# Two layers of a hybrid attention block: projection work spread evenly over the attention steps, some operations cut smaller, and the forget bias folded into a score product

## The chip, the cores and the metric

The kernel runs on one core of one Trainium2 chip. The metric is the time of one execution on the device in microseconds (us); before the change the median of three runs is 1368.33 us (1368.0 to 1369.17). One more execution was taken by the hardware profiler; its own time is 1369.85 us. The engines are called as in the profile: PE (matrix products; PEld is its loading of the stationary operand), DVE (vector), ACT (activations), POOL (GpSimd), SP (which here issues the transfers).

## The reference

Two layers over 512 tokens of width 1024, all in float32. Each layer is a mixer of three parallel head groups, then a gated MLP with a causal convolution:

```python
proj = h @ w_in      # split into fq fk fv ff | nq kc vc ks vs kw vw ng | dq dk dv
log_f = log_sigmoid(ff + b_forget); c = cumsum(log_f)
# forgetting attention ("fox"), 4 heads of width 64
s = q @ k.T * ATTN_SCALE + c_q[:, None] - c_k[None, :]
o_fox = masked_softmax(s, kpos <= qpos) @ v
# sparse attention, 8 heads: o = g0*compressed + g1*selected + g2*window
k_cmp = gelu(windows(kc) @ w1) @ w2          # the same for v_cmp
# dilated attention, 4 heads
mix = concat(o_fox, o_nsa, o_dil); x = x + rms_norm(mix @ w_out)
x = x + rms_norm((silu(conv(h @ w_up)[a]) * conv(h @ w_up)[b]) @ w_down)
```

The row term c_q drops out of a softmax, so a kernel needs only the term c_k, one value per head and key.

## The kernel before

**Numbers in two parts.** Every operand of a product is split into a high part, made by an ACT copy into a type of reduced precision, and a low part, made by a subtraction on DVE or POOL. A product is then three products on PE: high by high, low by high and high by low. `part_weights` (L137) does this for the weights: a weight tile `raw` arrives in one of three buffers, ACT writes `wh`, DVE or POOL writes `wl`. Names in `DCUTS` (L42: `w1`, `wo`) have each of the two operations cut in two along the slabs of the tile; the weights `wo2` (rows 512 to 1023 of the output projection, one slab of 1024 columns each) and the first weight of the MLP, `up` 0 0, are done in one operation of 1024 columns.

**The fox scores.** The query tile `q` of two heads holds the high part in partitions 0 to 63 and the low part in 64 to 127. The key tile `k` of a head holds the high part of the key twice (partitions 0 to 63 and 64 to 127) as plane 0 and the low part twice as plane 1 (`k_evac`, L494). So two products over 128 partitions give all terms. For fox heads a third product adds the forget bias: `esel` (a constant that picks a head) by `cst`, whose rows 0 to 3 and 32 to 35 hold the high and low parts of c for the four heads, the other rows zero:

```python
            mm(S[:, 0:n], qs, k[:, 0, 0:n], t != 1, False)
            mm(S[:, 0:n], qs, k[:, 1, 0:n], False, not fox)
            if fox:
                mm(S[:, 0:n], esel[:, u["h"], :], cst[:, 0:n], False, True)
```

`cst` is written once in a layer, by ACT and DVE (L612, L613), from a product `pcs` that stands on PE right after the projection of the fox queries (`fq_proj`, L594).

**Units, slots and pieces.** Attention is a pipeline of 96 units a layer: 16 fox units, 64 of the sparse group (8 heads, two branches), 16 dilated ones; a unit is one head, one branch and one block of 128 queries, and has 128, 256, 384 or 512 keys. One slot of the loop (L1238) starts one unit's scores and does later stages of earlier units: the masked minimum on DVE (1 slot later), the exponent on ACT, the normalization on POOL, the transposes on PE (4 slots), the copies `ph` on ACT and `pl` on DVE out of the transposes (5), the products with the values (7) and the head's output (7). Into the slots the loop puts pieces of other PE work, in a fixed order (`main_pieces`): 8 projections of 8 pieces (`kc`, `ks`, `nq0`, `kw`, `nq1`, `dv`, `dq`, `dk`), 8 pieces `w1` of the compression, and 16 pieces of the first half of the output projection (`out_first`), 88 in all. The second half (`out_start`) waits until the last unit has started, but each step in which it waits counts as a piece too. Five pieces go ahead of slot 0 (`FIRST`). Then a budget says how many follow in each slot; `until` calls more at once where a unit needs a projection that isn't there yet:

```python
        RATE = [1.4] * 12 + [0.8] * 98
...
                budget += RATE[i]
                while budget >= 1.0:
                    budget -= 1.0
                    if live[0] or pieces.late:
                        step()
                chain_step()
```

`chain_step` moves the compressed branch on by one stage a slot (`cmp_pieces`, L938): its gelu needs a reciprocal of 128x256 values, done as two operations of 128 columns in one stage (L952).

**Order.** PE's instructions keep the order in which the program writes them. DVE, ACT, POOL and SP are ordered by a planner at build time: by program order among what it expects to be ready. On the chip each engine then runs its list in that order and waits where an operand is late. Weight loads go out on SP as a raw buffer comes free. Large tiles (`q`, `k`, values, partial outputs) share 24 buffers (`NBIG`, L26). PSUM has two buffers `pt` for the transposes; a new transpose needs the copies `ph` and `pl` out of an older one to be done.

Of the kernel before, what the change touches and what calls it, by code (L numbers as in the profile page):

```python
# [10 lines left out]
F32R = mybir.dt.float32r  # L11
# [27 lines left out]
TT = "pt"  # L39
CT = "acc"  # L40
FIRST = 5
DCUTS = ("w1", "wo")  # L42
EV = (1, 3, 1, 1)
ORDER = (0, 1, 2, 4, 3, 5, 6, 7, 8)
HA0 = (1, 3)
# [29 lines left out]
def tile_hybrid_block(  # L75
# [61 lines left out]
    def part_weights(raw, nk, ncol, spare, tagn, pool, cut):  # L137
        DCUT = ((0, 2), (2, 4)) if cut else ((0, 4),)
        if spare:
            hi, lo = bt([128, nk, ncol], F32R, "wh"), bt([128, nk, ncol], F32R, "wl")  # L140
        else:
            hi = wpool.tile([128, nk, ncol], F32R, tag="wh", name=nm("wh" + tagn))
            lo = wpool.tile([128, nk, ncol], F32R, tag="wl", name=nm("wl" + tagn))
        for a, e in HCUT if pool else DCUT:
            ks = slice(nk * a // 4, nk * e // 4)
            nc.scalar.activation(hi[:, ks], raw[:, ks], AF.Copy)  # L146
        if pool:
            for a, e in PCUT:
                ks = slice(nk * a // 4, nk * e // 4)
                nc.gpsimd.tensor_sub(lo[:, ks], raw[:, ks], f(hi)[:, ks])  # L150
        else:
            for a, e in DCUT:
                ks = slice(nk * a // 4, nk * e // 4)
                nc.vector.tensor_sub(lo[:, ks], raw[:, ks], f(hi)[:, ks])  # L154
        return hi, lo

    plan, ready = [], {}
# [44 lines left out]
    def getw(*key, ahead=AHEAD, pre=None, peek=False):  # L202

        i = where[key]
        pre = ahead if pre is None else min(pre, ahead)
        tag = lambda k: "_".join(str(z) for z in k)
        for n in range(len(done)):
            upto = i + (ahead, pre)[n]
            while done[n] < len(plan) and done[n] <= upto:
                k, srcs, nk, ncol, spare = plan[done[n]]  # L210
                if n == 0:
                    ready[k] = load(srcs, nk, ncol, tag(k))
                else:
                    ready[k] = part_weights(ready[k], nk, ncol, spare, tag(k), k[1] in ONPOOL or k[1:4] in ONPOOL or k[0:3] in ONPOOL,
                                            k[1] in DCUTS)
                done[n] += 1
        return None if peek else ready.pop(key)

# [229 lines left out]
    for l in range(DEPTH):  # L448
# [42 lines left out]
                                               op0=ALU.mult, op1=ALU.subtract)  # L491
            return q

        def k_evac(p):  # L494
            k = bt([128, 2, 512], F32R, "k")
            nc.scalar.activation(k[:, 0, :], p, AF.Copy)
            nc.vector.tensor_sub(k[:, 1, :], p, f(k[:, 0, :]))
            return k

        def new_v(nh=2):  # L500
# [39 lines left out]
            tl.append(d.rearrange("p h u d -> p (h u d)"))  # L540
        tmode.__exit__(None, None, None)
        store["fv"] = fv
        store["fk"] = [k_evac(t_block(tl, 128 * j)) for j in range(4)]
        cpar = small.tile([128, 2, 88], F32, tag="cpar", bufs=1, name=nm("cpar"))
        crow = rt((88, 2, 128))
        for j in range(3):
# [47 lines left out]
        def fq_proj(c):  # L594
            hi, lo = getw(l, "fq", c, ahead=2)
            p = ps("acc")
            for k in range(KT):
                mm(p, hi[:, k, :], HH(k), k == 0, False)
                mm(p, hi[:, k, :], HL(k), False, False)
                mm(p, lo[:, k, :], HH(k), False, k == KT - 1)  # L600
            store["fq"].append(q_evac(p))

        fq_proj(0)
        fq_proj(1)
# [6 lines left out]
                       False, False)  # L611
        nc.scalar.activation(cst[0:4, :], pcs[0:4, :], AF.Copy)  # L612
        nc.vector.tensor_sub(cst[32:36, :], pcs[0:4, :], f(cst[0:4, :]))  # L613
        if l == 0:

            dint = rt(dt=I32)
            nc.gpsimd.iota(dint, pattern=[[-1, 512]], base=384, channel_multiplier=1)
            dflt = rt()
            nc.vector.tensor_copy(dflt, dint)
            cmask = const.tile([128, 512], F32, name="cmask")  # L620
            nc.vector.tensor_scalar(cmask, dflt, 0.0, BIG, op0=ALU.is_lt, op1=ALU.mult)
            dmask = const.tile([128, 512], F32, name="dmask")
            cnt = rt()
            nc.vector.tensor_scalar(cnt, dflt, 128.0, None, op0=ALU.is_le)
            for m in (3, 15):
                mi = rt(dt=I32)
                nc.vector.tensor_scalar(mi, dint, m, None, op0=ALU.bitwise_and)
                mf = rt()
                nc.vector.tensor_copy(mf, mi)
                nc.vector.scalar_tensor_tensor(cnt, mf, 0.0, cnt, op0=ALU.is_equal, op1=ALU.add)  # L630
            ge0 = rt()
            nc.vector.tensor_scalar(ge0, dflt, 0.0, None, op0=ALU.is_ge)
            nc.vector.tensor_mul(cnt, cnt, ge0)
            nc.vector.tensor_scalar(dmask, cnt, 0.0, BIG, op0=ALU.is_equal, op1=ALU.mult)
            for v, lg in ((2.0, -math.log(2.0)), (3.0, -math.log(3.0))):
                t = rt()
                nc.vector.tensor_scalar(t, cnt, v, lg, op0=ALU.is_equal, op1=ALU.mult)
                nc.vector.tensor_add(dmask, dmask, t)

            ci = rt((128, NST, 32))  # L640
            nc.gpsimd.iota(ci, pattern=[[128, NST], [-16, 32]], base=-31, channel_multiplier=1,
                           allow_small_or_imprecise_dtypes=True)
            cvalid = const.tile([128, NST, 32], F32, name="cvalid")
            nc.vector.tensor_scalar(cvalid, ci, 0.0, None, op0=ALU.is_ge)
            cinv = const.tile([128, NST, 32], F32, name="cinv")
            nc.vector.tensor_scalar(cinv, ci, 0.0, BIG, op0=ALU.is_lt, op1=ALU.mult)

            odd = const.tile([128, 2], F32, name="odd")
            oi = small.tile([128, 1], I32, tag="oi", bufs=1, name="oi")
            nc.gpsimd.iota(oi, pattern=[[0, 1]], base=0, channel_multiplier=1)  # L650
            nc.vector.tensor_scalar(oi, oi, 32, None, op0=ALU.bitwise_and)
            nc.vector.tensor_copy(odd[:, 1:2], oi)
            nc.vector.tensor_scalar(odd[:, 0:1], odd[:, 1:2], 0.0, None, op0=ALU.is_equal)
            nc.vector.tensor_scalar(odd[:, 1:2], odd[:, 1:2], 0.0, None, op0=ALU.is_gt)
            vcm = const.tile([128, 2, 2, 2, 64], F32R, name="vcm")
# [1 line left out]
        nc.vector.tensor_scalar(gates, gates, 1.0, None, op0=ALU.add)  # L657
        nc.vector.reciprocal(gates, gates)

        mix, sums = {}, {}  # L660
        OFIRST = (0, 1, 2, 3)

        def split_mix(k, eng, cs=slice(0, 512)):
            if k not in mix:
                if k != 7:
                    mix[k] = bt([128, 2, 512], F32R, "mix")
                else:
                    mix[k] = ptp.tile([128, 2, 512], F32R, tag="ph", name=nm("mix"))
            d = mix[k]
            nc.scalar.activation(d[:, 0, cs], sums[k][:, cs], AF.Copy)  # L670
            eng.tensor_sub(d[:, 1, cs], sums[k][:, cs], f(d[:, 0, cs]))

# [265 lines left out]
        def cmp_pieces(xc, w2r):  # L938
# [9 lines left out]
            nc.scalar.activation(t2, t1, AF.Exp, scale=-2.0 * math.sqrt(2.0 / math.pi))  # L948
            yield
            nc.vector.tensor_scalar(t2, t2, 1.0, None, op0=ALU.add)  # L950
            for c in range(2):
                nc.vector.reciprocal(t2[:, 128 * c:128 * c + 128], t2[:, 128 * c:128 * c + 128])  # L952
            yield
            nc.gpsimd.tensor_mul(xc, xc, t2)
            yield
            yield
# [146 lines left out]
        def st_scores(u):  # L1103
            t = u["t"]
            n = u["n"] = 128 * (t + 1)
            q, k, u["v"], u["mask"], u["gate"] = operands(u)
            if t != 1:
                state["s"] = ps("s")
            S = u["S"] = state["s"][:, 128 * (t == 1):]
            qs = q[:, 128 * t:128 * t + 128]  # L1110
            fox = u["grp"] == "f"
            mm(S[:, 0:n], qs, k[:, 0, 0:n], t != 1, False)
            mm(S[:, 0:n], qs, k[:, 1, 0:n], False, not fox)
            if fox:
                mm(S[:, 0:n], esel[:, u["h"], :], cst[:, 0:n], False, True)

        def st_max(u):
            n = u["n"]
# [109 lines left out]
                mm(p[:, sl], hi[:, k, :], HL(k)[:, sl], False, False)  # L1228
                mm(p[:, sl], lo[:, k, :], HH(k)[:, sl], False, last and k == KORDER[-1])

        RATE = [1.4] * 12 + [0.8] * 98
        LM, LN, LT, LE, LV, LO = LAGS
        stages = ((0, st_scores), (LE, st_keep_hi), (LM, st_max), (LN, st_norm), (LE, st_keep_lo), (LM, st_exp),
                  (LV, st_values), (LT, st_turn), (LO, st_out))
# [2 lines left out]
        with tc.manual_schedule(engines={mybir.EngineType.PE}):  # L1237
            for i in range(FIRST):  # L1238
                step()
            for i in range(len(units) + LO):  # L1240
                slot[0] = i
                U = lambda lag: units[i - lag] if 0 <= i - lag < len(units) else None
                for lag, fn in stages:
                    if U(lag) is not None:
                        fn(U(lag))
                budget += RATE[i]
                while budget >= 1.0:
                    budget -= 1.0
                    if live[0] or pieces.late:
                        step()  # L1250
                chain_step()
                if store.get("pc") and whole and whole[0][1] <= i:
                    cmp_values(whole.pop(0)[0])
# [169 lines left out]
```

## Time and profile before

| what | value |
|---|---|
| median of three runs | 1368.33 us |
| the profiled execution: its time, its span | 1369.85 us, 1367.9 us |
| PE, PEld busy | 98 %, 86 % of the span |
| DVE, ACT, POOL busy | 62 %, 53 %, 21 % |
| PE share of the chain of work that ended last | 85 % |
| mean granted clock of PE | 0.998 of full |
| the slots of layer 1, of layer 2 | 62 to 302 us, 737 to 979 us |

The span runs from the first to the last instruction of the program; 1.95 us of the profiled execution's time lie around it. A busy time is the time in which an instruction of that engine is under way. Products on PE overlap, so the time that one costs is the distance from its start to the start of the next, not its duration. The granted clock is a share of 2.4 GHz.

### The profile page before, as it was taken

The numbers are of one execution on the slowest core, as the hardware profiler recorded it, in microseconds if no ns is written. First come the engines' busy times: TensorE is split into PE (matmuls) and PEld (weight loads), VectorE is DVE, ScalarE is ACT, GpSimd is POOL, SyncE is SP. The second block draws the span as 40 slices with busy tenths as digits, with TensorE's granted clock in tenths as the row PEclk, the third lists the DMA queues.
The fourth block names the chain that finished last, engine by engine and source line by source line (L and its number), as shares of the span: only waits on it lengthen the run. The fifth ranks groups of instructions, "written<-read, shape, count | busy, mean of one in ns | idle before, by whom it ended". The sixth has DMA issues, their size and how long they took to land.

```text
span 1367.9 us, 21028 instructions
## 1 busy us (share of the span) xinstructions
PE 1338.0 (98%) x7855; PEld 1177.9 (86%) x7855; DVE 850.4 (62%) x1893; ACT 728.2 (53%) x1506; POOL 287.0 (21%) x343
## 2 busy tenths in 40 slices
PE   9999999999999999999999999999999999999997
PEld 8899998978888888888898999999798888888886
DVE  7677787677755555433464887777876555554334
ACT  6567767777533333333465677667774333333232
POOL 2364753341000000000004647634210000000000
PEclk9999999999999999999999999999999999999999
DMA  6323311131333333333333242111323333332231
GB/s 181 94 63 115 104 35 48 58 128 33 107 93 103 97 92 96 104 93 123 111 96 93 63 139 63 47 41 58 120 62 98 103 92 93 104 97 92 94 122 62
DMA packets 145517, 123.74 MB, mean 90 GB/s; under 512 B 8264, under 2 KB 135688, under 8 KB 145416
## 3 DMA queue, kind: packets, MB, share of 16 engines
q1 hardware_dynamic: 145416, 122.40, 29.5%
q8 instruction: 62, 1.02, 0.3%
q14 instruction: 39, 0.32, 0.1%
HBM read 118.19 MB, written 4.19 MB: 89 GB/s over the span
## 4 chain that ended last, share of the span: by engine, by line
PE 85%; DVE 7%; ACT 4%; POOL 2%; issue 2%; DMA 0%; SPq 0%; ACTq 0%; POOLq 0%; DVEq 0%
PE acc L115 39%; PE s L115 19%; PE pt L115 13%; PE o L115 10%; PE pt L1156 3%; POOL wt L795 1%; PE pt L737 1%; DVE hl L271 1%; DVE pl L1172 1%; DVE r L1126 1%; ACT r L1131 1%; DVE x L913 0%; ACT hh L270 0%; ACT h L310 0%; ACT ph L1167 0%
## 5 line engine op out<-in xcount | busy, mean ns | idle before, releaser
L154 DVE TENSOR_TENSOR wl_up<-raw_up,wh_up 128x1024 fp32r<-128x1024 f32 x78 | 95.6, 1225 | 170.8 <-ACT wh_up L146 170.8
L146 ACT ACTIVATE wh_up<-raw_up 128x1024 fp32r<-128x1024 f32 (+1 forms) x90 | 89.6, 1001 | 160.4 <-PE acc L115 68.1
L154 DVE TENSOR_TENSOR wl_wd<-raw_wd,wh_wd 128x1024 fp32r<-128x1024 f32 x42 | 51.5, 1225 | 133.7 <-ACT wh_wd L146 133.7
L146 ACT ACTIVATE wh_wd<-raw_wd 128x1024 fp32r<-128x1024 f32 x42 | 44.5, 1060 | 144.8 <-PE pt L115 135.5
L1143 POOL TENSOR_SCALAR r<-r,sm,gates 128x128 f32<-128x128 f32 (+3 forms) x128 | 86.4, 683 | 126.1 <-DVE sm L1139 82.3
L1131 ACT ACTIVATE r<-r,sm 128x128 f32<-128x128 f32 x192 | 106.7, 557 | 9.3 <-DVE sm L1126 8.4
L115 PE MATMUL acc<-hh,wl_up 128*128 128x512 f32 (+1 forms) x272 | 102.4, 376 | 0.0
L115 PE MATMUL acc<-hl,wh_up 128*128 128x512 f32 (+1 forms) x272 | 102.4, 376 | 0.0
L115 PE MATMUL acc<-hh,wh_up 128*128 128x512 f32 (+1 forms) x272 | 102.4, 376 | 0.0
L150 POOL TENSOR_TENSOR wl_kc<-raw_kc,wh_kc 128x512 fp32r<-128x512 f32 x8 | 11.8, 1490 | 417.6 <-ACT wh_kc L146 416.8
L115 PE MATMUL s<-k,q 128*128 128x512 f32 (+3 forms) x384 | 96.2, 337 | 0.6 <-DVE sm L1126 0.6
L1172 DVE TENSOR_TENSOR pl<-pt,ph 128x384 fp32r<-128x384 f32 x144 | 85.6, 596 | 17.3 <-ACT ph L1167 15.9
L1167 ACT ACTIVATE ph<-pt 128x384 fp32r<-128x384 f32 x144 | 75.4, 523 | 29.1 <-PE pt L1156 27.9
L1126 DVE CUSTOM_DVE_ANT_0 r<-s,cmask 128x128 f32<-128x128 f32 (+3 forms) x160 | 76.0, 482 | 20.6 <-PE s L115 16.2
L1156 PE MATMUL pt<-ident,r 128*128 128x128 f32 x480 | 77.5, 276 | 7.0 <-DVE pl L1172 5.5
L115 PE MATMUL acc<-wh_wd,gh 128*128 128x512 f32 x252 | 83.7, 389 | 0.0
L115 PE MATMUL s<-hh,wh_up 128*128 128x512 f32 (+1 forms) x224 | 80.4, 359 | 0.0
L115 PE MATMUL s<-hl,wh_up 128*128 128x512 f32 (+1 forms) x224 | 80.4, 359 | 0.0
L115 PE MATMUL s<-hh,wl_up 128*128 128x512 f32 (+1 forms) x224 | 80.4, 359 | 0.0
L1347 ACT ACTIVATE r<-r 128x512 f32<-128x512 f32 x44 | 27.8, 632 | 85.7 <-DVE r L1328 85.5
L1156 PEld LDWEIGHTS pt<-ident,r 128*128 128x128 f32 x480 | 55.4, 141 | 15.9 <-POOL r L1143 6.8
L115 PE MATMUL acc<-wh_wo,mix 128*128 128x256 f32 (+1 forms) x296 | 67.6, 305 | 0.0
(439 smaller groups left out, 4121.2 us busy)
## 6 DMA issues: line engine op xcount, KB each, us to landing
raw_up<-in_w_up_dram SPq DMA_DIRECT2D x88, 512.0 KB, 3.8
raw_wd<-in_w_down_dram SPq DMA_DIRECT2D x44, 512.0 KB, 3.4
raw_wo<-in_w_out_dram SPq DMA_DIRECT2D x16, 512.0 KB, 3.5
x<-in_x_dram SPq DMA_DIRECT2D x8, 512.0 KB, 5.9
raw_nq<-in_w_in_dram SPq DMA_DIRECT2D x8, 512.0 KB, 3.7
raw_w<-in_cmp_w_k_dram SPq DMA_DIRECT2D x8, 512.0 KB, 4.0
raw_w<-in_cmp_w_v_dram SPq DMA_DIRECT2D x8, 512.0 KB, 4.2
raw_fk<-in_w_in_dram SPq DMA_DIRECT2D x4, 512.0 KB, 5.9
```

The costliest lines, as they stand in the source:

```text
L115: nc.tensor.matmul(o, lhsT=lhsT, rhs=rhs, start=start, stop=stop, skip_group_check=True)
L146: nc.scalar.activation(hi[:, ks], raw[:, ks], AF.Copy)
L154: nc.vector.tensor_sub(lo[:, ks], raw[:, ks], f(hi)[:, ks])
L271: nc.vector.scalar_tensor_tensor(lo, src, gain[:, k:k + 1], f(hi), op0=ALU.mult, op1=ALU.subtract)
L737: nc.tensor.transpose(p[:, 128 * s:128 * s + 128], tl[s][:, 128 * j:128 * j + 128], ident)
L1126: nc.vector.tensor_tensor_reduce(row[:, 0:n], u["S"][:, 0:n], u["mask"][:, 512 - n:512], op0=ALU.add, op1=ALU.min, scale=1.0, scalar=3.0e3 ...
L1131: nc.scalar.activation(row[:, 0:n], row[:, 0:n], AF.Exp, scale=-1.0, bias=sm_[0], accum_out=sm_[1])
L1143: nc.gpsimd.tensor_scalar(row[:, 0:n], row[:, 0:n], z["sm"][2], g_, op0=ALU.mult, op1=ALU.mult)
L1156: nc.tensor.transpose(p[:, 128 * c:128 * c + 128], blocks[z], ident)
L1167: nc.scalar.activation(hi, src, AF.Copy)
L1172: nc.vector.tensor_sub(*u["lo"])
L1347: nc.scalar.activation(cd[0], cd[0], AF.Silu)
```

## The change

- The fox keys' low part is written in partitions 0 to 63 only (`k_evac(p, 64)`); 64 to 127 of plane 1 take a copy of rows 0 to 63 of `cst` by a transfer, one for each of the four heads. Two new large tiles `fq2` hold the high part of the query (copied by a transfer) in partitions 0 to 63 and `esel` of the head in 64 to 127 (two transfers each, which repeat a row of 128 values four times). The second score product of a fox unit takes `fq2`, and the third goes. The product of the two low parts, which the second had held for fox heads, goes with it.
- `RATE` is replaced: 1.4 for the first 12 slots as before, then the pieces that are left divided by the units that are left.
- `wo2` and `up` 0 are cut in two operations each on ACT and DVE; a tile of one slab is cut by columns.
- The reciprocal is done as four operations of 64 columns, one stage of the chain each.
- `kept` and `OLAG` are written and not used.

```diff
-DCUTS = ("w1", "wo")
+DCUTS = ("w1", "wo", "wo2")
...
+        def cutting(z, a, e):
+            return z[:, nk * a // 4:nk * e // 4] if nk > 1 else z[:, :, ncol * a // 4:ncol * e // 4]
+
         for a, e in HCUT if pool else DCUT:
...
+            nc.scalar.activation(cutting(hi, a, e), cutting(raw, a, e), AF.Copy)
+        for a, e in PCUT if pool else DCUT:
+            (nc.gpsimd if pool else nc.vector).tensor_sub(cutting(lo, a, e), cutting(raw, a, e), cutting(f(hi), a, e))
...
-                                            k[1] in DCUTS)
+                                            k[1] in DCUTS or k[1:3] == ("up", 0))
...
-        def k_evac(p):
+        def k_evac(p, low=128):
...
-            nc.vector.tensor_sub(k[:, 1, :], p, f(k[:, 0, :]))
+            nc.vector.tensor_sub(k[0:low, 1, :], p[0:low], f(k[0:low, 0, :]))
...
-        store["fk"] = [k_evac(t_block(tl, 128 * j)) for j in range(4)]
+        store["fk"] = [k_evac(t_block(tl, 128 * j), 64) for j in range(4)]
+        fq2 = [bt([128, 2, 512], F32R, "q2") for _ in range(2)]
...
-            store["fq"].append(q_evac(p))
+            q = q_evac(p)
+            store["fq"].append(q)
+            nc.sync.dma_start(f(fq2[c])[0:64], f(q)[0:64])
+            for j in range(2):
+                nc.sync.dma_start(f(fq2[c])[64:128, j].rearrange("p (t n) -> p t n", t=NST),
+                                  bc(f(esel)[0:64, 2 * c + j, :], 1, NST))
...
         nc.vector.tensor_sub(cst[32:36, :], pcs[0:4, :], f(cst[0:4, :]))
+        for k in store["fk"]:
+            nc.sync.dma_start(f(k)[64:128, 1, :], f(cst)[0:64, :])
...
-            for c in range(2):
-                nc.vector.reciprocal(t2[:, 128 * c:128 * c + 128], t2[:, 128 * c:128 * c + 128])
-            yield
+            for c in range(4):
+                nc.vector.reciprocal(t2[:, 64 * c:64 * c + 64], t2[:, 64 * c:64 * c + 64])
+                yield
...
-            fox = u["grp"] == "f"
             mm(S[:, 0:n], qs, k[:, 0, 0:n], t != 1, False)
-            mm(S[:, 0:n], qs, k[:, 1, 0:n], False, not fox)
-            if fox:
-                mm(S[:, 0:n], esel[:, u["h"], :], cst[:, 0:n], False, True)
+            if u["grp"] == "f":
+                qs = fq2[u["h"] // 2][:, u["h"] % 2, 128 * t:128 * t + 128]
+            mm(S[:, 0:n], qs, k[:, 1, 0:n], False, True)
...
-        RATE = [1.4] * 12 + [0.8] * 98
+
+        NPIECES = 8 * 8 + 2 * 4 + 16
...
-                budget += RATE[i]
+                budget += 1.4 if i < 12 else max(NPIECES - pieces.n, 0.8) / max(len(units) - i, 1)
```

## Rows read from the trace of the kernel before

**Rows 1.** The page's first part: busy time, share of the span, instructions.
```profile
PE 1338.0 (98%) x7855; PEld 1177.9 (86%) x7855; DVE 850.4 (62%) x1893; ACT 728.2 (53%) x1506; POOL 287.0 (21%) x343
```
**Rows 2.** Stretches from:to, length, busy time of each engine, granted clock, DMA share, GB/s.
```profile
62.30:112.10 49.80, 49.25 (x392) 47.69 (x391) 35.27 (x109) 31.73 (x90) 30.45 (x32) 1.00 0.23 65
130.80:271.40 140.60, 136.63 (x1058) 130.00 (x1057) 106.54 (x331) 101.06 (x267) 73.67 (x95) 1.00 0.20 62
161.00:166.30 5.30, 3.48 (x27) 2.93 (x25) 4.99 (x13) 4.41 (x11) 2.83 (x6) 1.00 0.46 124
271.40:290.20 18.80, 16.79 (x116) 14.63 (x114) 15.21 (x54) 16.20 (x47) 10.40 (x16) 1.00 0.29 85
805.40:947.40 142.00, 138.00 (x1058) 131.39 (x1056) 106.53 (x331) 101.11 (x267) 73.36 (x95) 0.99 0.20 61
893.00:899.00 6.00, 5.47 (x30) 5.21 (x30) 3.59 (x10) 3.07 (x8) 2.27 (x3) 0.72 0.25 90
947.40:966.20 18.80, 16.78 (x115) 14.62 (x114) 15.24 (x54) 16.14 (x46) 10.36 (x16) 1.00 0.27 84
```
**Rows 3.** The tile cst: the product that it feeds; duration min/median/max, first and last start.
```profile
L115 PE MATMUL s<-cst,esel x32: 273/308/397, 62.5 to 780.0; 128*128 128x128 f32 x8, 128*128 128x256 f32 x8, 128*128 128x384 f32 x8, 128*128 128x512 f32 x8
```
**Rows 4.** PE in order of time in the first slots: start, length, line, product, count.
```profile
62.49 0.27 PE L115 MATMUL s<-cst,esel 128*128 128x128 f32 x1
62.60 0.34 PE L115 MATMUL acc<-wh_kc,hh 128*128 128x256 f32 x1
...
69.74 0.40 PE L115 MATMUL s<-cst,esel 128*128 128x512 f32 x1
69.97 0.28 PE L115 MATMUL acc<-wh_ks,hh 128*128 128x256 f32 x1
```
**Rows 5.** The chain of waits: the last piece of the output projection's first half.
```profile
271.73 1.48 PE acc L115 x12
```
**Rows 6.** PE in order of time: products that waited; in brackets idle time, releaser.
```profile
166.27 0.52 PE L1156 MATMUL pt<-ident,r 128*128 128x128 f32 x3 [1.52 <-DVE pl L1172]
277.63 0.52 PE L1156 MATMUL pt<-ident,r 128*128 128x128 f32 x3 [0.57 <-DVE pl L1172]
281.81 0.50 PE L115 MATMUL pt<-pch,vcm 64*128 64x512 f32 x1 [0.80 <-DVE pl L1172]
287.69 0.52 PE L1156 MATMUL pt<-ident,r 128*128 128x128 f32 x3 [0.65 <-DVE pl L1172]
295.74 0.50 PE L115 MATMUL o<-pl,v 128*128 128x512 f32 x1 [1.06 <-DVE pl L1172]
```
**Rows 7.** DVE in order of time, where PE waited.
```profile
162.29 1.76 DVE L952 RECIPROCAL r<-r 128x128 f32<-128x128 f32 x2
293.60 1.48 DVE L154 TENSOR_TENSOR wl<-raw_wo,wh 128x1024 fp32r<-128x1024 f32 x1 [0.52 <-ACT wh L146]
295.00 0.68 DVE L1172 TENSOR_TENSOR pl<-pt,ph 128x512 fp32r<-128x512 f32 x1
```
**Rows 8.** Groups of DVE's instructions by shape: busy us, mean ns of one.
```profile
L154 DVE TENSOR_TENSOR wl_wo<-raw_wo,wh_wo 128x512 fp32r<-128x512 f32 x16 | 10.8, 684 | 0.7 <-ACT wh_wo L146 0.5
L154 DVE TENSOR_TENSOR wl_wo<-raw_wo,wh_wo 128x1024 fp32r<-128x1024 f32 x4 | 4.9, 1226 | 2.5 <-ACT wh_wo L146 2.5
L658 DVE RECIPROCAL gates<-gates 128x96 f32<-128x96 f32 x2 | 1.5, 742 | 0.0
L584 DVE RECIPROCAL fl<-fl 128x16 f32<-128x16 f32 x2 | 0.5, 253 | 1.7 <-ACT fl L581 1.7
```
**Rows 9.** The write of cst (durations in ns, first and last start in us).
```profile
L613 DVE TENSOR_TENSOR cst<-acc,cst x2: 679/680/680, 57.2 to 731.9; 4x512 fp32r<-4x512 f32 x2
```
**Rows 10.** SP in order of time: the next load after cst is written.
```profile
64.40 0.37 SPq L134 DMA_DIRECT2D raw_kw<-in_w_in_dram  x1
```
**Rows 11.** Transfers by line: count, KB each, median us from issue to landing.
```profile
raw_ks<-in_w_in_dram SPq DMA_DIRECT2D x4, 512.0 KB, 4.7
w2r<-in_cmp_w_k_dram SPq DMA_DIRECT2D x2, 64.0 KB, 2.6
```

More of the change, by code (lines that the diff above doesn't have):

```diff
@@ L143, in part_weights @@
             lo = wpool.tile([128, nk, ncol], F32R, tag="wl", name=nm("wl" + tagn))
+        def cutting(z, a, e):
+            return z[:, nk * a // 4:nk * e // 4] if nk > 1 else z[:, :, ncol * a // 4:ncol * e // 4]
         for a, e in HCUT if pool else DCUT:
[L145 to L154, printed above, removed]
+            nc.scalar.activation(cutting(hi, a, e), cutting(raw, a, e), AF.Copy)
+        for a, e in PCUT if pool else DCUT:
+            (nc.gpsimd if pool else nc.vector).tensor_sub(cutting(lo, a, e), cutting(raw, a, e), cutting(f(hi), a, e))
         return hi, lo
@@ L658, in tile_hybrid_block @@
         nc.vector.reciprocal(gates, gates)
-        mix, sums = {}, {}
+        mix, sums, kept = {}, {}, {}
         OFIRST = (0, 1, 2, 3)
+        OLAG = 200
         def split_mix(k, eng, cs=slice(0, 512)):
@@ L669, in split_mix @@
             d = mix[k]
+            kept[k] = slot[0]
             nc.scalar.activation(d[:, 0, cs], sums[k][:, cs], AF.Copy)
```

## The prediction

> **What bounds the kernel now.** First the busy times: PE is busy 98 % of the span, DVE 62 %, ACT 53 % [rows 1]. A busy PE can still be one that waits inside overlapping products, so next the distances from start to start: in the first slots a product of 128 columns is followed by the next after 0.11 us (62.49 to 62.60), one of 512 columns after 0.23 (69.74 to 69.97) [rows 4], and a piece of twelve products of 256 columns takes 1.48, 0.12 each [rows 5]. That is columns at 2.4 GHz and little more: where nothing waits, PE sets the time, and a product taken away is time gained. Then the stretches [rows 2], to see where PE does wait. In the fox slots (62.3 to 112.1) it idles 0.55 us. From slot 20 to slot 80 (130.8 to 271.4) it idles 3.97, of which 1.82 lie between 161.0 and 166.3. From slot 80 to 95 (271.4 to 290.2) it idles 2.01 of 18.8 while ACT is busy 86 % and DVE 81 %: these slots have no pieces, and the latency of ACT and DVE paces them. The second layer repeats the first 674.6 us later (130.8 and 805.4 are the same slot).
>
> **The fox product.** 32 products go [rows 3]: eight each of 128, 256, 384 and 512 columns, at 0.11, 0.12, 0.17 (between its neighbours) and 0.23 us. 8 x 0.63 = **-5.0 us**. PE hardly idles there, so nothing hides it; the bounds are -3.5 (if a third comes back as waits on DVE, which is 71 % busy there) and -5.0. The second product keeps its columns, and the half-height low part of the key saves DVE nothing I can see in a row: 0.
>
> **The copies.** Each layer gains ten transfers, 2 x (256 + 128 + 128) + 4 x 128 KB = 1.5 MB, all on SP, 0.37 us of issue each [rows 10], where SP next has a load to issue at 64.40. What ends last is the copy of `cst` into the first key. `cst` is complete at 57.2 + 0.68 = 57.9 [rows 9]; the copy is needed by the second product of slot 0, just before 62.49 [rows 4]. No row shows a transfer from one SBUF tile to another. The nearest are 2.6 us for 64 KB and 4.7 for 512 KB [rows 11]: it lands between 60.5 and 62.6, so the wait is 0 to 0.2 us; queued behind one other 512 KB it is up to 4.9. The first case is nearest, since 128 KB is nearer to 64, but the query's copies and a weight load are in the queue at the same time: I take 0.5 a layer, **+1.0**. What hides the rest is the five pieces ahead of slot 0. The later heads' copies have four slots each in hand. Behind a waiting copy stand SP's weight loads, which run several pieces ahead.
>
> [...]
>
> **The even spread.** Counted through the loop: 5 pieces ahead and 16 by slot 11, 24 by slot 15; unit 16 calls 4 at once and unit 20 calls 7, so 39 are done after slot 20. At 0.8 a slot the 88th falls in slot 80, and the 14 slots after it get steps that do nothing. The trace agrees: the last piece starts at 271.73 [rows 5]. After the change 48 pieces are left at slot 20 for 76 slots, 0.63 each, and the 88th falls in slot 95. About nine pieces, 9 x 1.48 = 13 us of PE work, move behind slot 80. PE's three waits there, 0.57 + 0.80 + 0.65 = 2.02 [rows 6], are all for `pl` on DVE, one of the two copies that free a transpose buffer; with 13 us more of PE work in the same slots that copy is done in time. I take all of it, 2 x 2.0 = **-4.0** (bounds 0 and -5.0, the refill after each wait counted). The price is in slots 20 to 80: 140.6 us become about 127 with at most a little less DVE work than 106.5, so DVE goes from 76 % to some 82 %. New waits of 0 to 2 us a layer; I take 0.5, **+1.0**.
>
> **The reciprocal.** Two operations hold DVE from 162.29 for 1.76 us [rows 7]; `pl` behind them is late, and PE waits 1.52 [rows 6]. One of 64 columns lies between those of 16 and 96, 0.25 and 0.74 us [rows 8]: 0.54. In that slot DVE is held 1.2 us less, and PE's wait shrinks by as much; the other three quarters come a slot apart, where 0.54 us is hidden by PE's piece. The compressed branch ends three slots later and later still by the thinner pieces, but its first consumer is the output projection, which now starts near slot 71. 2 x 1.2 = **-2.4** (bounds 0 and -3.6, all of the idle time of that stretch).
>
> **The cut weights.** At 293.60 DVE starts one `wl` of 1.48 us; a `pl` that stands behind it starts at 295.00, and PE waits 1.06 for it [rows 6, 7]. Two halves cost 2 x 0.68 against 1.23 [rows 8], 0.14 more, but either `pl` gets in between, or the first half starts when half of ACT's copy is done. 2 x 0.6 = **-1.2** (bounds +0.3 and -2.1). The other `wo2` and `up` 0 stand where no PE wait is laid to them: 0.
>
> **The sum:** -5.0 + 1.0 - 4.0 + 1.0 - 2.4 - 1.2 = -10.6 us. Against the profiled execution, 1367.9 of span and 1.95 around it, 1369.85, that gives 1359.3; the median of the runs is 1.5 lower, so I forecast **1357.7 us**.
>
> **Rivals.** *The even spread gives back what it takes.* For it: DVE at 82 % in slots 20 to 80 is as busy as it is in the slots that wait now (81 %). Against it: there PE has pieces to do while DVE catches up. Then only the fox product is sure: -5.0 + 1.0, half of the reciprocal -1.2, 0 for the rest: 1363.1.
>
> *All waits go.* -5.0 with no wait for copies, -5.0, -3.6 and -2.1, and the clock: between 893.0 and 899.0 PE was granted 0.72 on average, a time at 1.2 GHz after a row of waits, and slots 20 to 80 take 142.0 us in layer 2 against 140.6 [rows 2], so 1.4 more. -17.1: 1351.2.
>
> *The copy of `cst` stands behind a load on SP (slower).* If the planner puts the load of `raw_kw`, which goes out at 64.40 when a raw buffer comes free [rows 10], ahead of the copy, the copy is issued at 64.8 and lands at 67.4 to 69.5 [rows 11]. PE's order is fixed, so it stands from 62.4: 5.0 to 7.1 us, and with the clock lost as above 1.4 more, in both layers up to 17 against -11.6 for the rest: about 1373. It decides from a landing at 66.8 on. Against it: `cst` is ready 6.5 us ahead of that load. [...]
>
> *The change does not do what it says:* `until` could call so many pieces that none are left to spread. The count above excludes it.
>
> **How the numbers follow.** Forecast 0.57 (its own range 1354 to 1361), give-back 0.18, all waits 0.12, the slow copy 0.07, and 0.06 for a sum of small new waits that leaves 1366 to 1370. A measurement of this kernel can tell about 0.2 %, 2.7 us, from no change. Faster, below 1365.6: 0.86; within: 0.08; slower, above 1371.1: 0.06. The range 1350 to 1365 takes in the first three cases but for their edges.
>
> **What would show it.** Right: no product of `cst` by `esel`, the slot 0 score of a fox unit at about 62.4 with no wait; pieces up to about slot 95, and no PE wait for `pl` in the dilated slots; reciprocals a slot apart; `wl` halves before the last units' `pl`. Wrong: an idle PE before the second product of slot 0, more PE idle time than 4 us a layer between slots 20 and 80, or waits for `pl` that only moved.

## The result: slower, and where the time went

The changed kernel takes **1383.07 us** (median of 5 runs, 1381.49 to 1383.68) against 1368.33 of the kernel before: ratio 1.0098, 95% interval 1.0084 to 1.0111. The forecast was 1357.7, faster. The profiled execution's span is 1379.7 us, 11.8 more than before. It took 1381.49 us, the least of the five, and that of the kernel before 1369.85, 1.5 above its median, so what follows places those 11.8 us and not the whole 14.7 by which the medians differ.

The page's first part, as in [rows 1]:

```profile
PE 1337.6 (97%) x7823; PEld 1176.7 (85%) x7823; DVE 856.4 (62%) x1907; ACT 729.9 (53%) x1516; POOL 284.7 (21%) x343
```

The 32 products are gone (7855 to 7823) and PE is still busy 97 % of a longer span. So again distances are what to read. Stretches of the kernel after, columns as in [rows 2]: the fox slots of both layers, slots 20 to 80, and slots 80 to 95.

```profile
63.00:113.30 50.30, 47.50 (x378) 45.43 (x376) 35.00 (x109) 31.50 (x90) 30.32 (x32) 1.00 0.24 69
131.90:266.60 134.70, 125.78 (x951) 118.39 (x949) 104.39 (x330) 95.70 (x254) 71.00 (x94) 0.99 0.19 57
266.60:294.20 27.60, 27.60 (x213) 26.30 (x210) 20.73 (x63) 21.24 (x61) 10.24 (x17) 1.00 0.18 54
742.50:794.90 52.40, 49.00 (x377) 46.95 (x375) 35.03 (x109) 31.44 (x89) 30.29 (x32) 0.97 0.24 68
```

Slots 80 to 95 did what was forecast: PE idles 0.00 of 27.6 us, where it idled 2.01 of 18.8 [rows 2], and no wait of [rows 6] is left there. But the fox slots, with 2.5 us of products less a layer, take 50.3 and 52.4 us instead of 49.8, and slots 20 to 80 idle 8.9 us instead of 3.97. The view of PE's waits over the whole span (us in total, times, longest) says where to look:

```profile
PE acc L1046 <- DVE pcl L1054: 8.7, 4, 3.7
PE s L115 <- DMA k<-cst: 3.7, 2, 2.2
PE pt L744 <- DVE pl L1178: 3.1, 4, 1.1
PE pt L744 <- DVE q L486: 2.6, 2, 1.3
PE pt L1162 <- DVE k L493: 2.4, 2, 1.2
```

Before, no wait for `k<-cst` could exist, and the one for `pcl`, the low part of the compressed branch's probabilities, was 1.3 in all:

```profile
PE acc L1039 <- DVE pcl L1047: 1.3, 2, 0.7
```

To place the loss, take for each product of PE the distance to the next start, less what it takes where nothing waits (0.11 us for 128 columns, 0.12 for 256, 0.23 for 512: [rows 4, 5]), and sum it by slots. Us a layer, mean of the two layers (two numbers: layers 1 and 2), for the kernels below (e1 to f4 are the experiments of the next section). Only differences between kernels count: what is taken for the smallest products moves the levels, and in the kernel after about 1 us may be counted to either side of slot 48.

```
slots        before    after     e1    e2    e6    e8   e10       f3    f4
0-3          0.0     1.8/3.9    0.0   4.2   0.0   4.1   0.0      0.0   0.0
4-15         1.3       2.5      1.3   2.5   1.3   2.5   2.5      1.3   2.5
16-47        2.8       4.9      5.4   2.8   6.1   5.4   2.8      2.8   2.4
48-55        3.0       6.4      3.1   3.0   7.7   3.1   2.9      3.0   3.0
56-63      0.8/2.3     1.6      0.8   2.4   0.8   0.8  0.9/2.4  0.8/2.3 0.9/2.4
64-79        1.0       1.9      1.9   1.0   1.0   1.9   1.0      2.5   2.5
80-94        3.2       0.5      0.5   3.4   3.2   0.5   3.2      0.8   0.8
60 us after  4.3       4.5      4.4   4.2   4.3   4.5   4.3      3.8   3.8
```

Over the whole span this excess grows from 45.6 to 62.2 us, +16.6; the products removed give -5.0; together +11.6 of the 11.8.

**At slot 0.** PE in order of time in the kernel after (start, length, line, product; in brackets the idle time and its releaser), and SP's issues:

```profile
62.97 0.22 PE L115 MATMUL s<-k,q 128*128 128x128 f32 x1
64.74 0.33 PE L115 MATMUL s<-k,q 128*128 128x128 f32 x1 [1.55 <-DMA k<-cst]
```
```profile
57.70 0.37 SPq L134 DMA_DIRECT2D raw_nq<-in_w_in_dram  x1
58.17 0.70 SPq L601 DMA_DIRECT2D q<-q  x1
58.96 3.01 SPq L618 DMA_DIRECT2D k<-cst  x4
65.01 0.37 SPq L134 DMA_DIRECT2D raw_kw<-in_w_in_dram  x1
```

The first key's copy is issued at 58.96, 0.5 us after `cst` is complete (58.4), and the product that needs it starts 5.8 us later. Ahead of it stand a load, but of `raw_nq`, and the copy of the queries; `raw_kw`, the load of my rival, comes after. Behind this wait of 1.55 us the granted clock stays at 1.00 (first row of the stretches above); in layer 2 the wait is 2.2 and the stretch has 0.97, and the table has 1.8 and 3.9 for the two.

**At slots 48 to 55.** PE, POOL and DVE of the kernel after around its longest wait, then the stretch behind it:

```profile
202.69 0.49 PE L1162 MATMUL pt<-ident,r 128*128 128x128 f32 x3
206.92 0.66 PE L1046 MATMUL acc<-ident,r 128*128 128x128 f32 x2 [3.73 <-DVE pcl L1054]
```
```profile
202.49 1.27 POOL L150 TENSOR_TENSOR wl_dk<-raw_dk,wh_dk 128x512 fp32r<-128x512 f32 x1
203.75 0.77 POOL L1149 TENSOR_SCALAR r<-r,sm,gates 128x512 f32<-128x512 f32 x1
204.48 0.61 POOL L1040 TENSOR_TENSOR r<-r,sm 128x256 f32<-128x256 f32 x1
205.05 0.72 POOL L1035 TENSOR_TENSOR r<-r,cvalid 128x256 f32<-128x256 f32 x1
```
```profile
205.81 0.42 DVE L1036 TENSOR_REDUCE sm<-r 128x8 f32<-128x256 f32 x1 [2.02 <-POOL r L1035]
206.35 0.42 DVE L1054 TENSOR_TENSOR pcl<-acc,pch 128x256 fp32r<-128x256 f32 x1
```
```profile
207.00:211.00 4.00, 4.00 (x20) 3.81 (x21) 1.65 (x9) 1.56 (x5) 1.60 (x3) 0.64 0.42 131
```

The next transposes of the compressed branch stand in PE's fixed order. They wait for an `acc` buffer that `pcl` must free; the branch's masking (L1035) stands on POOL behind half of the split of `wl_dk` and two normalisations; DVE waits 2.02 us for it before it can sum the rows (L1036), and `pcl` stands behind that sum on DVE's list. After these 3.7 us without work, the granted clock of the next 4 us is 0.64: it is 0.50 in every half microsecond from 206.5 to 209.5, where a product of 512 columns takes 0.42 us (208.02 to 208.44) instead of 0.23.

### The profile page after: what moved, and what is told of

Read it like the earlier page. It is cut to its first block, busy times and chain, and to the rows that moved or that the text cites. A ratio compares the mean times of both kernels' runs of the same rounds, so it can differ in the third digit from the quotient of the medians.

```text
span 1379.7 us, 21036 instructions
## 1 busy us (share of the span) xinstructions
PE 1337.6 (97%) x7823; PEld 1176.7 (85%) x7823; DVE 856.4 (62%) x1907; ACT 729.9 (53%) x1516; POOL 284.7 (21%) x343
## 3 DMA queue, kind: packets, MB, share of 16 engines
q8 instruction: 62, 1.02, 0.3%
## 4 chain that ended last, share of the span: by engine, by line
PE 80%; DVE 8%; ACT 5%; POOL 3%; issue 2%; DMA 1%; SPq 0%; ACTq 0%; POOLq 0%; DVEq 0%
PE acc L115 35%; PE s L115 18%; PE pt L115 12%; PE o L115 10%; PE pt L1162 3%; DVE wt L802 1%; DMA k<-cst 1%; DVE hl L267 1%; PE pt L744 1%; DVE r L1132 1%; POOL wl_dq L150 1%; POOL r L1149 1%; DVE pl L1178 1%; ACT r L1137 1%; POOL wl_dv L150 1%
## 5 line engine op out<-in xcount | busy, mean ns | idle before, releaser
L1149 POOL TENSOR_SCALAR r<-r,sm,gates 128x128 f32<-128x128 f32 (+3 forms) x128 | 83.3, 659 | 114.2 <-DVE sm L1145 67.9
L150 POOL TENSOR_TENSOR wl_kc<-raw_kc,wh_kc 128x512 fp32r<-128x512 f32 x8 | 11.8, 1484 | 417.5 <-ACT wh_kc L148 416.7
```

What stands on the lines that cost most here:

```text
L150: (nc.gpsimd if pool else nc.vector).tensor_sub(cutting(lo, a, e), cutting(raw, a, e), cutting(f(hi), a, e))
L1149: nc.gpsimd.tensor_scalar(row[:, 0:n], row[:, 0:n], z["sm"][2], g_, op0=ALU.mult, op1=ALU.mult)
```

## The experiments

Each has its own runs of the kernel before beside it: median 1368.1 (e1 to e4), 1368.8 (e5 to e8), 1368.3 (e9 to e12), 1369.0 (f1 to f4), 1368.4 (f5).

### One part at a time

e1, the kernel before with the even spread:
```
-                budget += RATE[i]
+                budget += 1.4 if i < 12 else max(NPIECES - pieces.n, 0.8) / max(len(units) - i, 1)
```


> The kernel before with the even spread alone (14 PE pieces spread to slot 95, nothing else changed). Theory A (the thinner pieces shorten slots 32 to 56, while the stages of the compressed branch are counted in slots, so its transposes on PE stand before pcl is written): slower, 1371 to 1377 us, with a PE wait of over 2 us for pcl in each layer and products at half the rate behind it, and the waits for pl in slots 80 to 95 gone. Theory B (the spread is sound and the copies cost the time): 1363 to 1367 us as forecast, no wait for pcl over 1 us.

Measured 1370.29, ratio 1.0017 (1.0007 to 1.0026): slower by 2.2 us, where the forecast had 3.0 faster. Between the two theories: the waits for `pcl` appear but the longest is 1.1 us. PE's largest waits between slots 20 and 95 of layer 1:

```profile
PE acc L1039 <- DVE pcl L1047: 1.6, 2, 1.1
PE pt L737 <- DVE q L490: 1.3, 1, 1.3
PE pt L1156 <- DVE k L497: 1.2, 1, 1.2
PE pt L1156 <- DVE pl L1172: 1.0, 2, 0.8
```

The table has the sum: 80 to 94 gives 2.7 us a layer, 16 to 47 takes 2.6 and 64 to 79 0.9.

e2, the kernel before with the fold (copies and half-height low part as in the change, not printed again):
```
-            mm(S[:, 0:n], qs, k[:, 1, 0:n], False, not fox)
-            if fox:
-                mm(S[:, 0:n], esel[:, u["h"], :], cst[:, 0:n], False, True)
+            if u["grp"] == "f":
+                qs = fq2[u["h"] // 2][:, u["h"] % 2, 128 * t:128 * t + 128]
+            mm(S[:, 0:n], qs, k[:, 1, 0:n], False, True)
```


> The kernel before with the forget bias taken along in the second product alone (old spread, old weight cuts, old reciprocal). Theory B (the copies of cst into the keys land late and stop PE at slot 0, 1.7 us in layer 1 and 3.6 in layer 2, clock included): 1367 to 1370 us, the 5.0 us of the products eaten. Theory A (the loss is the spread's): the copies cost about the 1 us that was forecast, 1363 to 1365 us.

Measured 1374.73, 1.0050 (1.0034 to 1.0066): worse than either. In the profiled execution, of 1378.16 us, PE stands at slot 0, and the stretch behind it was granted 0.72:

```profile
65.47 0.33 PE L115 MATMUL s<-k,q 128*128 128x128 f32 x1 [2.20 <-DMA k<-cst]
```
```profile
66.00:72.00 6.00, 6.00 (x39) 6.00 (x38) 1.87 (x11) 1.74 (x8) 0.73 (x2) 0.72 0.32 87
```

So a wait of 2.2 costs 3.9, since part of the products after it run at about half the rate: from 66.21 to 67.92 those of 256 columns follow one another after 0.21 us instead of 0.12. In layer 2, 2.7 costs 4.4.

e3, the change with the old budget (the edit of e1 undone), and e4, the kernel before with the small operations:
```
-            for c in range(2):
-                nc.vector.reciprocal(t2[:, 128 * c:128 * c + 128], t2[:, 128 * c:128 * c + 128])
-            yield
+            for c in range(4):
+                nc.vector.reciprocal(t2[:, 64 * c:64 * c + 64], t2[:, 64 * c:64 * c + 64])
+                yield
-DCUTS = ("w1", "wo")
+DCUTS = ("w1", "wo", "wo2")
...
```


> The changed kernel with the old budget of pieces (1.4 a slot to slot 12, then 0.8), so the fold and the smaller operations without the even spread. Theory A: the wait for pcl is gone or under 1 us, 1362 to 1367 us. Theory B: the copies still cost 5 us, 1364 to 1369 us. Theory C (the four-stage reciprocal puts the compressed branch three slots later, behind weight halves on POOL): the wait for pcl stays, 1370 us or more.

> The kernel before with the smaller operations alone: wo2 and the first up weights cut in two, the reciprocal in four stages a slot apart. Forecast of the prediction for these: -3.6 us, 1364 to 1366 us. Theory C (three slots later is what makes the compressed branch late): slower, 1370 us or more, with a PE wait for pcl over 2 us a layer. Theory A alone: no such wait with the old spread, and 1364 to 1368 us.

Measured e3 1388.96, 1.0151 (1.0136 to 1.0166); e4 1381.56, 1.0098 (1.0083 to 1.0113). Theory A falls as the main cause: without the spread the change is slower still, and the small operations, for which my bounds allowed a loss of 0.3 us at most, cost 13.5 us alone.

### Which of the small operations

e5 has the cuts alone; e6 has neither, but three stages that do nothing; e7 the four reciprocals in the old number of stages; e8 the change with e7's loop.
```
             nc.gpsimd.tensor_mul(xc, xc, t2)
             yield
             yield
+            for c in range(3):          # e6
+                yield
...
             for c in range(4):          # e7, e8
                 nc.vector.reciprocal(t2[:, 64 * c:64 * c + 64], t2[:, 64 * c:64 * c + 64])
+                if c == 1:
                     yield
```


> The kernel before with the cut weights alone (wo2 and the first up weights in halves). The small operations together cost 13.5 us. Theory C (the reciprocal in four stages is the whole loss, by the slot in which the compressed branch comes): 1366 to 1369 us here. Theory D (the cuts reorder what the planner puts on ACT and DVE at the end of the attention and cost there): 1371 us or more.

> The kernel before with three idle stages put behind the reciprocal (its two operations as before), so that everything behind it in the compressed branch is issued three slots later and nothing else changes. Theory C: the PE waits for an acc buffer behind rope (1.9 us) and behind the compressed scores (1.5 us) appear, 1378 to 1386 us. If the pieces of the reciprocal themselves cost the time: 1368 us, give or take 1.

> The kernel before with the reciprocal in four parts, two to a slot, in the number of slots that it had, so the rest of the compressed branch is issued in the slots of before. Theory C: the shorter hold of DVE is kept and no new wait comes, 1364.5 to 1367.5 us. If the operations of 64 columns cost more than they free: 1369 us or more.

> The changed kernel with the reciprocal in four parts, two to a slot, in the number of slots of before. Theory C: the waits for pcl (3.7 us and what follows) shrink to those of the even spread alone, under 1.5 us each; what is left over the kernel before is the copies, 1368 to 1374 us. If the late compressed branch isn't due to the three stages: 1380 us or more.

Measured: e5 1369.65, 1.0003 (0.9994 to 1.0013); e6 1383.16, 1.0106 (1.0091 to 1.0121); e7 1369.13, 0.9999 (0.9990 to 1.0008); e8 1376.69, 1.0057 (1.0040 to 1.0073). Theory C stands for the loss: three stages of nothing cost 14.4 us. (The planner makes its lists anew for e6, so the order on DVE, ACT and POOL may have moved with the slots; the runs don't separate the two.) Of the change's own loss they are 1383.1 - 1376.7 = 6.4; the spread puts the branch against other slots, so the price is another. e8 lies above its forecast of 1368 to 1374: the longest wait for `pcl` is back to 1.1 us as in e1, but the copies cost 4.1 us a layer (table), more than I had counted. What e6 waits for, PE and then DVE:

```profile
191.54 1.28 PE L115 MATMUL acc<-kcm,q 128*128 128x64 f32 x8 [1.47 <-DVE r L1020]
201.07 1.05 PE L115 MATMUL acc<-kcm,q 128*128 128x64 f32 x8 [1.94 <-DVE acc L473]
213.49 0.41 PE L1041 MATMUL acc<-ident,r 128*128 128x128 f32 x2 [0.99 <-DVE r L476]
```
```profile
199.17 0.23 DVE L471 TENSOR_TENSOR rope<-acc,ss 128x64 f32<-128x64 f32 x1 [1.33 <-PE acc L115]
199.43 0.23 DVE L473 TENSOR_TENSOR acc<-acc,cc 128x64 f32<-128x64 f32 x1
```

The branch's scores take an `acc` buffer, of which there are three, and here the one they get holds a query piece that PE has only just finished: DVE must rotate it first. In the old slots the two didn't meet.

The gains of both operations fell short. In its profile e7's shorter hold of DVE takes 0.4 us off the wait of [rows 6] (1.52 to 1.10): POOL's multiplication, which needs all four parts, is late next. Its times show no gain. In e5 the two halves run back to back, 1.98 us where the one operation took 1.48 [rows 7], and `pl` still stands behind both; PE waits 1.11 instead of 1.06. PE of e7; DVE of e5, PE of e5:

```profile
165.81 0.52 PE L1157 MATMUL pt<-ident,r 128*128 128x128 f32 x3 [1.10 <-POOL r L955]
```
```profile
294.80 1.98 DVE L150 TENSOR_TENSOR wl<-raw_wo,wh 128x512 fp32r<-128x512 f32 x2
296.70 0.68 DVE L1168 TENSOR_TENSOR pl<-pt,ph 128x512 fp32r<-128x512 f32 x1
```
```profile
297.43 0.50 PE L115 MATMUL o<-pl,v 128*128 128x512 f32 x1 [1.11 <-DVE pl L1168]
```

### The copies

e9 is e2 with the keys' copies on ACT's queue; e10 is e2 with every copy done by an engine; f1 is e10 with the keys' copies as DMAs on SP, f5 with the first key's alone.
```
-            nc.sync.dma_start(f(k)[64:128, 1, :], f(cst)[0:64, :])
+            nc.scalar.dma_start(f(k)[64:128, 1, :], f(cst)[0:64, :])       # e9
+            (nc.gpsimd if i else nc.vector).tensor_copy(k[64:128, 1, :], cst[0:64, :])   # e10
...
-            nc.sync.dma_start(f(fq2[c])[0:64], f(q)[0:64])
+            nc.gpsimd.tensor_copy(fq2[c][0:64], q[0:64])                   # e10, f1, f5; esel alike
```


> The fold alone as in e2, but the four copies of cst into the keys issued from ACT's DMA queue; the copies of q and esel stay on SP's. Theory E (the copy is late because it stands in SP's rings behind 512 KB of raw_nq and the copies of q): landing within 3 us of issue, PE's wait at slot 0 under 0.5 us, 1366 to 1370 us. Theory F (a copy between SBUF tiles takes 5 us and more wherever it is issued, or the DMA engines are shared and full): the waits of 2.2 and 2.7 us stay, 1373 us or more.

> The fold alone, with every copy done by an engine instead of a DMA: the first key's by DVE, the other keys', q's and esel's by POOL. If the copies' DMA latency is all that eats the 5.0 us of the products: no wait at slot 0, 1363 to 1366 us. If POOL, at some 1.3 us for 512 columns, is late instead: a wait for POOL at slot 0, 1367 us or more.

> The fold alone with the four copies of cst into the keys as DMAs on SP's queue, but the copies of q and esel done by POOL. Theory E (the key's copy is late because the copies of q and esel and a weight load share the DMA engines with it): it lands within 3.5 us of issue and PE waits under 0.5 us at slot 0, 1366 to 1368.5 us. Theory F (a 128 KB copy between SBUF tiles takes 5 us by itself): the waits of 2.2 and 2.7 us stay, 1372 us or more.

> As f1 (q, esel by POOL), but only the first key's copy of cst is a DMA; the other three keys' are done by POOL. Theory E2 (the four copies of f1 run interleaved at some 200 GB/s and land together, so that the first waits for 0.38 MB of the others, 1.9 us): it lands about 62.8 us in layer 1, PE waits under 0.4 us at slot 0, 1366 to 1368.5 us. Theory E3 (what it waits for is the 512 KB of raw_nq issued 0.5 us ahead of it): PE's waits of 1.7 and 1.2 us stay, 1369 us or more.

Measured: e9 1374.18 (1369.92 to 1377.65), 1.0037 (1.0025 to 1.0048). Its profile has no wait in layer 1 and one of 2.36 us in layer 2, but the profiled execution took 1369.92 us, 4.3 less than the median, and isn't typical: inconclusive as to the wait. By the median, 0.6 from that of e2, another queue doesn't keep the copy out of the way. e10 1366.12, **0.9983** (0.9974 to 0.9993): the fold is a gain once no DMA is in it, and the copies as DMAs cost 1374.7 - 1366.1 = 8.6 us. (e10 keeps the two new large tiles, so their hold on the 24 shared buffers isn't what costs.) f1 1371.30, 1.0018 (1.0008 to 1.0028), waits 1.7 and 1.2; f5 1369.43, 1.0005 (0.9995 to 1.0014), waits 0.8 and 0.4 in its profiled execution, of 1367.67 us. So both theories hold in part: in the profiles the two layers' waits together go from 4.9 us (e2) to 2.9 without the copies of `q` and `esel` as DMAs (f1) and to 1.2 without the three other keys' too (f5). The rest is the load ahead. In f5 the two can be told apart by the size of their packets, 1 KB for the load of `raw_nq` and 2 KB for the key's copy, which is issued at 59.19. PE, and the packets from 59.70 to 61.65 and from 61.65 to 62.50:

```profile
63.20 0.30 PE L115 MATMUL s<-k,q 128*128 128x128 f32 x1 [0.79 <-DMA k<-cst]
```
```profile
DMA packets 429, 0.44 MB, mean 225 GB/s; under 512 B 0, under 2 KB 429, under 8 KB 429
DMA packets 179, 0.22 MB, mean 254 GB/s; under 512 B 32, under 2 KB 115, under 8 KB 179
```

For 2.5 of its 4.0 us the copy has moved nothing: up to 61.65 every packet is the load's. All 64 packets of the copy (179 - 115) follow within 0.85 us, beside the load's last 83. What the four keys' copies of f1 move, first mostly beside the load and then alone (last two columns: share of the DMA engines' time, GB/s):

```profile
61.00:62.40 1.40, 1.40 (x14) 1.39 (x12) 0.00 (x0) 1.15 (x2) 0.57 (x1) 1.00 1.02 334
62.80:64.40 1.60, 0.19 (x2) 0.22 (x3) 0.00 (x0) 0.00 (x0) 1.53 (x2) 1.00 0.95 182
```

Both stretches have the DMA engines full (1.02 and 0.95), the first at 334 GB/s and the second at 182. If all ten copies pass at 182, the 1.5 MB (1573 KB in thousands of bytes) keep them for 8.6 us a layer, an estimate from this one stretch; that this is also the time that the copies cost in all is chance. Why the copies pass more slowly isn't shown: the load also comes from DRAM and fills 128 partitions, the copies come from another tile and fill 64, and no run separates the two.

Engines do the same for little; POOL, DVE and PE's waits (slots 0 to 20) in e10:

```profile
54.72 1.03 POOL L604 CAST q<-q 64x1024 fp32r<-64x1024 f32 x1 [1.44 <-ACT q L489]
60.84 1.73 POOL L621 CAST k<-cst 64x512 fp32r<-64x512 f32 x3
```
```profile
58.79 1.09 DVE L621 CAST k<-cst 64x512 fp32r<-64x512 f32 x1
```
```profile
PE pt L745 <- DVE pl L1179: 1.1, 1, 1.1
```

In the kernel before, the same wait was:

```profile
PE pt L737 <- DVE pl L1172: 0.5, 1, 0.5
```

With it the excess of slots 4 to 15 grows by 1.2 us a layer in the table: with less to do there, PE catches up with DVE. These 2.4 us are most of why the fold gives 2.2 and not 5.0.

### The spread, and the whole

e11 begins the spread at slot 56, e12 adds e10's fold; f2 is the change with e8's reciprocal and e10's copies; f3 begins the spread at slot 70; f4 is f3 with e10's fold and e7's reciprocal.
```
-                budget += RATE[i]
+                budget += 1.4 if i < 12 else 0.8 if i < 70 else max(NPIECES - pieces.n, 0.8) / max(len(units) - i, 1)
```


> The kernel before with the spread begun at slot 56, behind the compressed branch's last stage, so that slots 12 to 55 keep 0.8 pieces each and the 20 pieces that are left are spread over slots 56 to 95. Theory A (the thinner slots 20 to 56 cost what the filled slots 80 to 95 save): the gain of the last stretch is kept without the price, 1363 to 1366 us. If the price lies in slots 56 to 95 instead: 1368 us or more.

> The fold with the copies by engines (e10) and the late spread (e11) together, old reciprocal and old weight cuts: the sum of the two if both theories hold, 1359 to 1363 us; if the fold's copies still stop PE at slot 0, 1364 us or more.

> The whole change with two repairs: the copies by engines instead of DMAs, and the reciprocal in four parts in the number of slots of before. If the causes add up (1376.7 us with the reciprocal repaired, less the 8.6 us by which the copies by engines beat the DMAs): 1366.5 to 1369.5 us, what is left being the spread's own price. If they don't, something else in the change costs: 1371 us or more.

> The kernel before with the spread begun at slot 70, when the last key of the dilated heads has been written and only output-projection pieces, which need no transpose buffer, are left. Theory A2 (the spread's price is that the pieces with queries and keys come later and their copies on DVE hold the two transpose buffers against the scores' own transposes): the gain of slots 80 to 95 without the price, 1363.5 to 1366.5 us. Theory G (every thinner slot waits for DVE, whatever its pieces are): 1368 us or more.

> The fold with the copies by engines, the reciprocal in four parts in the slots of before, and the spread from slot 70. By theory A2 the gains add up: 1366.1 less 0.8 for the reciprocal less 3 for the spread, 1361.5 to 1364.5 us. By theory G: 1366 us or more.

Measured: e11 1373.38, 1.0031 (1.0019 to 1.0042), e12 1370.92, 1.0014 (1.0005 to 1.0023): both slower than forecast. By the working of the table, e11 gains 1.9 us a layer in slots 80 to 94 but loses 4.3 in 64 to 79, in waits for `pl` and the keys (PE's waits from slot 60 on):

```profile
PE pt L1156 <- DVE pl L1172: 2.0, 2, 1.3
PE pt L115 <- DVE k L497: 1.0, 1, 1.0
```

f2 1368.00, 0.9995 (0.9986 to 1.0005): as added up, so with the copies, the stages and the spread's price nothing of the loss is left over. f3 1365.44, **0.9979** (0.9969 to 0.9988); f4 **1363.95, 0.9961 (0.9947 to 0.9975)**, faster than both kernels. PE's waits from slot 60 on in f3:

```profile
PE pt L115 <- DVE pl L1172: 0.9, 2, 0.7
PE acc L115 <- ACT part L852: 0.7, 1, 0.7
PE pt L1156 <- DVE sm L1139: 0.6, 1, 0.6
```

Theory A2 stands where G would have had 1368: pieces of the output projection can be thinned at a price of 1.5 us a layer against a gain of 2.4; pieces with queries and keys, whose transposes share the two `pt` buffers with the scores', cost more than they bring (3.5 against 2.7 in e1, 4.3 against 1.9 in e11). That the buffer, and not DVE's load in those slots, decides is argued from the waits' names, and e1's largest is for an `acc` buffer; no run with another buffer was made.

## Why the prediction was wrong

Two of its signs of being wrong came: PE idle before the second product of slot 0, and 8.9 us of idle time between slots 20 and 80.

- **The fox product.** -5.0 holds for the products taken away; 2.4 come back as waits on DVE. The bound for that, -3.5, was too hopeful: e10 gives -2.2. "Columns at 2.4 GHz and little more" holds for 256 columns (0.12 us, where 2.4 columns a nanosecond would give 0.11) and 512 (0.23 and 0.21); 128 columns would be 0.05 us, and the row had 0.11. The sum used the row, so it stands. That full speed is 2.4 GHz is worked out from the trace of before: at a granted clock of 0.50, from 895.08 to 897.00, nine products of 256 columns take 0.213 us each, 1.2 columns a nanosecond.
- **The copies** failed by size: "I take 0.5 a layer, +1.0" measured 8.6 alone and 5.6 in the profile of the change (slots 0 to 3; 8.2 in e8, which has the same copies). I took "the first case is nearest", a copy with nothing ahead of it; "queued behind one other 512 KB it is up to 4.9" was the near case. Load and copies share the DMA engines: in f5 the copy stands 2.5 us behind the load, and four keys' copies together pass at 182 GB/s. My rival had the mechanism (a load ahead) with the wrong load; in layer 1 the copy was never as late as its 66.8 (64.7 in the change, 65.5 in e2), and the time still rose, since the other terms failed too.
- **The even spread**: -4.0 forecast, -5.4 in slots 80 to 94; its price, "I take 0.5, +1.0", measured 2.6 + 0.9 a layer, 7.0. I priced it by DVE's mean load; by their names, the waits come where a piece's evacuation meets the scores' transposes. The give-back rival had the outcome, but not by its reason: it had DVE at 82 % in slots 20 to 80, and in the change that is 77 % (104.39 of 134.70).
- **The reciprocal** is where the argument broke, and the largest miss (-2.4 against +5.5 in the last item's sum): "The compressed branch ends three slots later and later still by the thinner pieces, but its first consumer is the output projection". The branch's own products stand in PE's fixed order and its buffers are shared with the pieces: +14.4 alone (e6), +6.4 in the change. Of -2.4, 0.8 is in e7's profile, and its times (0.9990 to 1.0008) don't show it.
- **The cut weights**: -1.2 forecast, nothing measured; neither halving's effect occurred.
- The sum for the profile: -5.0 + 2.4 + 5.6, the spread +2.0 (e1 against before, slots 16 to 55 and from 64 on), the stages +5.5 (slots 16 to 55, after against e8), and 0.7 ahead of slot 0 of layer 1: 11.2 of the 11.6 us that the excess and the removed products come to. The 3 us more by which the medians differ are not placed; that the copies are some 2.6 of them is an estimate from e8 (8.2 against 5.6).

## What to carry to other kernels

Where an engine's order is fixed, a stage that moves by some slots meets other holders of its buffers, even if nobody needs its result yet (14.4 us for three stages in e6): list the buffers and engines of every instruction moved, not only its last consumer. A small DMA just ahead of a deadline is priced by what shares the DMA engines with it (in f5 4.0 us for 128 KB issued right behind a load); where an idle engine can do the copy in 1 us (1.09 on DVE in e10), it should. When slots are made even, look at what kind of work is thinned (a price of 1.5 us a layer in f3, 4.3 in e11).

## What the hardware showed unexpectedly

In the profile of before the same 125 products, slots 56 to 63, take 16.6 us in layer 1 and 18.0 in layer 2:

```profile
218.40:235.00 16.60, 16.08 (x125) 15.46 (x125) 13.10 (x43) 11.60 (x30) 5.23 (x7) 1.00 0.15 51
893.00:911.00 18.00, 17.47 (x125) 16.86 (x125) 13.06 (x43) 11.56 (x29) 5.21 (x7) 0.91 0.14 43
```

PE's idle time is the same (0.52 and 0.53); the granted clock is 1.00 and 0.91, and the fall lies between 893 and 899 (0.72, [rows 2]). The table shows the step in one layer or both of e2, e10, f3 and f4 and in none of e1, e6 and e8, so 1.4 us a layer of any comparison here can be this step. What decides it stays open.
